# Seven products instead of eight for the columns of v, taken in turns with the plain blocks of the input projection

## The chip, the cores and the metric

The kernel runs on one core of one Trainium2 chip. The metric is device time in microseconds (us); lower is better. A kernel's time is the median of its runs, and one further execution is profiled. Engines are named as in the profile: PE is TensorE's matmuls and PEld its weight loads, DVE is VectorE, ACT is ScalarE, POOL is GpSimd, and SP is the engine whose queue issues most of the transfers.

## What is computed

One decoder block on x of 256 x 2048, all in float32. Cut to what matters here:

```python
proj = x @ w_in
b_gate, c_gate, u, q, k, v, r, z_low = split(proj)   # 1024, 1024, 1024, 512, 512, 1024, 1024, 16 columns

y_conv = group_rms_norm(b_gate * causal_conv3(c_gate * u), conv_norm_g)
z      = z_low @ w_gate_up + gate_bias
log_a  = log_sigmoid(z) / 16
o      = chunked_linear_attention(q, k, v, log_a)     # 4 heads, chunks of 64
y_gla  = group_rms_norm(o, gla_norm_g) * silu(r)

x = layer_norm(alpha * x + concat(y_conv, y_gla) @ w_out)
x = layer_norm(alpha * x + square(relu(x @ w_ff_up)) @ w_ff_down)
```

## The kernel before, in words

**Products in three.** The 256 rows are two tiles (t = 0, 1) of 128. A float32 product is made of three products of the chip's float32r type: each operand is split into a rounded part and the remainder (`split`, L110: a copy on ACT, L111, and a subtraction on DVE, L112), and PE adds high x high, high x low and low x high (`products`, L154, the matmuls at L164, L165, L166). Weights come in chunks of two slices of K (of 128 rows each) by at most 512 columns. `raw_chunk` (L142) takes a slot of the pool `raw` (13 slots, `RAWS`) and loads it on SP's queue (L115); `parts_of` (L123) splits it into a slot of the pool `hl` (5 slots, `HL`). PE then does 2 x 3 matmuls with it for each of the two row tiles.

**The input projection.** `block` (L317) makes one block of columns: 8 chunks, 96 matmuls, with one accumulator bank per row tile (six banks in all, `accp`), and hands each finished bank to a function (`done`). The columns are laid out by `IN_COLS` and `IN_BLOCKS` (L57 to L59): q, k, the 16 columns for the gates and v stand first, 2064 columns in five blocks of 412 or 414 (`qkvz`, L344; blocks 0 to 4, tiles ps_p). Then come c, u and b for the first half of the convolution's channels, c, u and b for the second half, and r, each a block of 512 (L565 to L571 and L589; tiles ps_c, ps_u, ps_b, ps_r). Block 0 also loads and splits x, and there the order on PE, ACT, DVE and SP is forced by hand (`queue`, L370); for block 1 it stays forced on ACT and DVE, after which `queue` is cleared (L383).

**The order of later work.** A list, `lag0.soon`, holds pieces of work with a count. After every group of matmuls (one chunk for one row tile) the counts go down by one (`Lagged.after`, L181), and a piece whose count is used up is issued behind that group. Everything else is ordered by the compiler's scheduler.

**Gates.** `gates` (L324) runs for each row tile when block 2 ends: small copies on ACT, a transposition on PE (pz), a copy, a matmul (z), three activations on ACT (Abs, Exp, Ln) and one operation on DVE, all issued at once.

**Attention.** `gla(t)` (L431) is a generator with four pieces: running sums of the decays on PE (bc, be, bt at L440), exponentials on ACT (L445, L446, L449, L452) and products on DVE (L447 to L453); transpositions (pqk, L462) with copies on ACT; the scores (pss, pso) and the state (pst); and the outputs (po) with their norm. The pieces are put on the list behind the last block of v, with the counts of `GLA_WAIT` (L48, L511 to L514), so they run beside the first c block, c0.

**Convolution.** The c block is copied to SBUF (`done_c`, L529). When u is there, `done_u` (L533) multiplies it with c, writes the product to a pad in DRAM (L539) and reads it back twice, shifted by one and two rows (L540, L541). All three transfers are issued on ACT's queue. The product tile has one buffer for both row tiles. DVE then weighs and adds the three (L542 to L546). `done_b` (L548) multiplies with b and normalizes.

**The up and down stage.** `up` (L760) already makes 1024 columns of the up projection by a Strassen scheme (the Winograd variant): the operands are cut in halves, rows by row tile, K by 1024 and columns by 512. Seven products of half size, in four accumulator banks a, b, c and d, replace eight. Each product is 4 steps (chunks) of 6 matmuls. The left operands are x1's parts or sums of them, made beforehand; the right ones are raw chunks or sums of them, which DVE makes in place in the slots r11, r12, r21, r22 (L774, L779, L783, L791). The chunks of the down projection are taken in between, four for every seven steps.

Of the kernel before, what the change touches and what calls it, by code (L numbers as in the profile page):

```python
# [10 lines left out]
F32 = mybir.dt.float32  # L11
# [45 lines left out]
IN_COLS = [(C_Q, NB), (C_K, NB), (C_Z, RANK), (C_V, 2 * NB),  # L57
           (C_C, NB), (C_U, NB), (C_B, NB), (C_C + NB, NB), (C_U + NB, NB), (C_B + NB, NB), (C_R, 2 * NB)]
# [4 lines left out]
def hymba_block(ctx, tc, x, x_t, w_in, conv_w, conv_g, w_gate, gate_b, gla_g, w_out,  # L63
# [207 lines left out]

    mixT = {}


    with ExitStack() as p1:
# [36 lines left out]
        vs = [keep.tile([P, HEADS, HV], F32, name=f"v_{t}") for t in range(NT)]  # L312
        las = [keep.tile([P, HEADS * HK], F32, name=f"la_{t}") for t in range(NT)]
# [10 lines left out]
        def gates(t, zl_ps):  # L324
            nc.scalar.copy(zparts[:, 0, :RANK], zl_ps)
            nc.scalar.copy(zparts[:, 1, :RANK], zl_ps)
            nc.vector.tensor_sub(zparts[:, 2, :RANK], zl_ps, zparts[:, 0, :RANK].bitcast(F32))
            pz = misc_tile(f"pz_{t}")
            nc.tensor.transpose(pz[:3 * ZP, :P], flat(zparts.bitcast(F32)), ident)
            nc.scalar.copy(zlT, pz[:3 * ZP, :P])  # L330
            z = misc_tile(f"z_{t}")
            nc.tensor.matmul(z, zlT, wgu, start=True, stop=True)
            e = las[t]
            nc.scalar.activation(e, z, AF.Abs)
            nc.scalar.activation(e, e, AF.Exp, scale=-1.0)
            nc.scalar.activation(e, e, AF.Ln, bias=one_b)
            nc.vector.scalar_tensor_tensor(las[t], z, 0.0, e, op0=ALU.min, op1=ALU.subtract)
# [6 lines left out]
        def qkvz(i):  # L344
# [8 lines left out]
            def done(t, ps):  # L353
                def go():
                    for what, d0, p0, n in pieces:
                        src = ps[:, p0:p0 + n]
                        if what == 2:
                            gates(t, src)
                        else:
                            dst = flat(vs[t]) if what == 3 else qk[t][:, what, :]  # L360
                            queued("act", lambda: nc.scalar.copy(dst[:, d0:d0 + n], src))
# [9 lines left out]
        at, ncol, done, name = qkvz(0)  # L371
# [3 lines left out]
        del queue["pe"], queue["sync"]  # L375
# [4 lines left out]


        block(*qkvz(1))
        queue.clear()  # L383


        once = tp8.tile([P, D], F32, tag="t8", name="once")
        wraw, ones, rest = once[:, 0:HEADS * HK], once[:, D - P:], once[:, D - 2 * P:D - P]
# [33 lines left out]
        for i in range(2, len(widths)):  # L421
            block(*qkvz(i))
# [98 lines left out]
        def conv_block(j):  # L521
            c_sb, h_sb = {}, {}
# [6 lines left out]
            def done_c(t, ps):  # L529
                c_sb[t] = cv.tile([P, NB], F32, tag="c", name=f"c_{j}_{t}")  # L530
                nc.scalar.copy(c_sb[t], ps)

            def done_u(t, ps):  # L533
                y = c_sb[t]
# [13 lines left out]
            def done_b(t, ps):  # L548
                y = c_sb[t]
# [13 lines left out]
            return done_c, done_u, done_b  # L563
# [28 lines left out]
    with ExitStack() as p2:  # L592
# [132 lines left out]

        KH = KT // 2
# [23 lines left out]
        def of_sum(what):  # L757
            return lambda kt: (sums[what][:, 0, kt, :], sums[what][:, 1, kt, :])

        def up(g, hT):  # L760

            n1, n2 = g * GROUP, g * GROUP + NB
            r11, r12, r21, r22 = {}, {}, {}, {}

            def raw(at, half, j, name):
                return raw_chunk(w_up, KH * half + KC * j, at, NB, f"{name}_{g}_{j}")

            def first(j):
                r11[j] = raw(n1, 0, j, "r11")
                return r11[j]  # L770

            def first_sum(j):
                r12[j] = raw(n2, 0, j, "r12")
                nc.vector.tensor_add(r11[j], r11[j], r12[j])  # L774
                return r11[j]

            def third_sum(j):
                r22[j] = raw(n2, 1, j, "r22")
                nc.vector.tensor_add(r12[j], r12[j], r22[j])  # L779
                return r12[j]  # L780

            def second_sum(j):
                nc.vector.tensor_add(r11[j], r11[j], r22[j])  # L783
                return r11[j]

            def last(j):
                r21[j] = raw(n1, 1, j, "r21")
                return r21[j]

            def fourth_sum(j):  # L790
                nc.vector.tensor_add(r11[j], r11[j], r21[j])  # L791
                return r11[j]

            def tmp(name):
                return cp.tile([P, NB], F32, tag="c", name=f"{name}_{g}")

            banks, kept = {}, {}

            def out(x, i, t, where=None):
                hidden(x if where is None else where, x, hT, i, t, f"h{g}_{i}_{t}", WAIT_UP)  # L800

            def end_1():
                kept["p1"] = tmp("p1")
                nc.scalar.copy(kept["p1"], banks["a"])

            def end_2():
                out(banks["a"], 0, 0, ht.tile([P, NB], F32, tag="relu", name=f"relu_{g}"))

            def end_6():
                kept["u"], kept["v"] = tmp("u"), tmp("v")  # L810
                nc.vector.tensor_sub(kept["u"], banks["b"], kept["p1"])
                nc.vector.tensor_sub(kept["v"], banks["c"], kept["u"])
                nc.vector.tensor_sub(kept["v"], kept["v"], banks["d"])
                out(kept["v"], 1, 1)

            def end_3():
                x = tmp("x12")
                nc.vector.tensor_sub(x, kept["u"], banks["c"])
                out(x, 1, 0)

            def end_4():
                nc.vector.tensor_add(kept["u"], banks["d"], kept["u"])
                out(kept["u"], 0, 1)

            plan = [(first, of_x1(0, 0), "a", end_1),
                    (first_sum, of_sum("s1"), "c", None),
                    (third_sum, of_sum("s3"), "d", None),
                    (second_sum, of_sum("q"), "b", end_6),
                    (lambda j: r22[j], of_sum("s4"), "c", end_3),
                    (last, of_x1(1, 0), "a", end_2),  # L830
                    (fourth_sum, of_x1(1, 1), "d", end_4)]
            n = KH // KC
            steps = [(p, j) for p in range(len(plan)) for j in range(n)]
            ready = {}

            def prepare(s):
                if s < len(steps):
                    p, j = steps[s]
# [158 lines left out]
```

## Time and profile before

| | |
|---|---|
| median of 3 runs | 1074.92 us (1074.33 to 1074.92) |
| the profiled execution, its own time | 1074.74 us |
| its span, first to last instruction | 1073.0 us |
| granted TensorE clock, mean | 0.997 |
| blocks 0 to 4 (q, k, gates, v) | 5.0 to 98.3 us |
| c0 with the attention beside it | 98.3 to 138.1 us |
| the other blocks up to the first of r | 138.1 to 247.8 us |

How to read the profile: "busy" is the time in which an engine works on an instruction; matmuls are pipelined, so that a matmul's own duration is longer than the time from one to the next. A group line names line, engine, operation, out<-in by the program's names, shapes and count, then busy time and the mean ns of one, then the idle time of the engine ahead of them and what ended it. A row of the windows gives a stretch in us from the span's start, its length, the busy time of each engine with the number of instructions, the granted clock, the share of the transfer engines and GB/s. A line of the timeline gives start, duration, engine and operation, and in brackets the idle time before it. A q behind an engine's name is its queue of issued transfers. Releasers are inferred from semaphores; a wait for several is put down to the one that came last.

### The profile page before, as it was taken

The numbers are of one execution on the slowest core, as the hardware profiler recorded it, in microseconds if no ns is written. First come the engines' busy times: TensorE is split into PE (matmuls) and PEld (weight loads), VectorE is DVE, ScalarE is ACT, GpSimd is POOL, SyncE is SP. The second block draws the span as 40 slices with busy tenths as digits, with TensorE's granted clock in tenths as the row PEclk, the third lists the DMA queues.
The fourth block names the chain that finished last, engine by engine and source line by source line (L and its number), as shares of the span: only waits on it lengthen the run. The fifth ranks groups of instructions, "written<-read, shape, count | busy, mean of one in ns | idle before, by whom it ended". The sixth has DMA issues, their size and how long they took to land.

```text
span 1073.0 us, 13204 instructions
## 1 busy us (share of the span) xinstructions
PE 1057.5 (99%) x4876; PEld 888.0 (83%) x4876; DVE 886.4 (83%) x1017; ACT 590.7 (55%) x685; POOL 1.4 (0%) x9
## 2 busy tenths in 40 slices
PE   9999999999999999999999999999999999999995
PEld 8999888888888878888888888888888888888885
DVE  6555557668565599999999999999999999999857
ACT  6575554434653356766556556556556656656620
POOL 0000000000000000000000000000000000000000
PEclk9999999999999999999999999999999999999998
DMA  9976358677686346366576566567567468367802
GB/s 334 317 241 215 117 160 277 202 222 229 191 335 192 118 149 243 99 230 221 176 230 213 185 208 223 175 201 234 168 196 259 137 198 274 120 201 256 299 27 78
DMA packets 69430, 218.69 MB, mean 204 GB/s; under 512 B 7219, under 2 KB 18243, under 8 KB 69110
## 3 DMA queue, kind: packets, MB, share of 16 engines
q1 hardware_dynamic: 64656, 206.87, 58.6%
q10 hardware_dynamic: 4710, 10.99, 2.9%
q8 instruction: 38, 0.62, 0.2%
q14 instruction: 26, 0.21, 0.1%
HBM read 214.67 MB, written 3.15 MB: 203 GB/s over the span
## 4 chain that ended last, share of the span: by engine, by line
PE 93%; DVE 4%; ACT 1%; issue 1%; DMA 1%; DVEq 0%; ACTq 0%
PE ps_dn L166 11%; PE ps_dn L165 10%; PE ps_dn L164 10%; PE ps_p L166 3%; PE ps_p L164 3%; PE ps_p L165 3%; PE ps_o L165 2%; PE ps_o L166 2%; PE ps_o L164 2%; PE ps_upa L164 2%; PE ps_upc L164 2%; PE ps_upa L166 2%; PE ps_upa L165 2%; PE ps_upc L166 2%; PE ps_upc L165 2%; PE ps_upd L164 2%
## 5 line engine op out<-in xcount | busy, mean ns | idle before, releaser
L111 ACT CAST hl_up<-raw_r 128x1024 fp32r<-128x1024 f32 x196 | 206.4, 1055 | 130.1 <-PE ps_dn L166 65.7
L112 DVE TENSOR_TENSOR hl_up<-raw_r,hl_up 128x1024 fp32r<-128x1024 f32 x196 | 237.0, 1219 | 9.8 <-ACT hl_up L111 9.3
L111 ACT CAST hl_dn<-raw_dn 128x1024 fp32r<-128x1024 f32 x128 | 134.5, 1054 | 117.5 <-PE ps_dn L166 96.9
L164 PE MATMUL ps_dn<-hl_dn,hT_hi 128*128 128x512 f32 x496 | 193.5, 391 | 0.0
L166 PE MATMUL ps_dn<-hl_dn,hT_lo 128*128 128x512 f32 x496 | 193.1, 389 | 0.0
L165 PE MATMUL ps_dn<-hl_dn,hT_hi 128*128 128x512 f32 x496 | 193.0, 389 | 0.0
L112 DVE TENSOR_TENSOR hl_dn<-raw_dn,hl_dn 128x1024 fp32r<-128x1024 f32 x128 | 155.8, 1220 | 16.1 <-ACT hl_dn L111 15.4
L166 PEld LDWEIGHTS ps_dn<-hl_dn,hT_lo 128*128 128x128 f32 x496 | 93.1, 188 | 19.6
L165 PEld LDWEIGHTS ps_dn<-hl_dn,hT_hi 128*128 128x128 f32 x496 | 93.1, 188 | 19.2
L164 PEld LDWEIGHTS ps_dn<-hl_dn,hT_hi 128*128 128x128 f32 x496 | 93.1, 188 | 19.1
L112 DVE TENSOR_TENSOR hl_o<-raw_o,hl_o 128x1024 fp32r<-128x1024 f32 x32 | 38.5, 1223 | 30.9 <-ACT hl_o L111 30.7
L112 DVE TENSOR_TENSOR hl_p<-raw_p,hl_p 128x824 fp32r<-128x824 f32 (+1 forms) x38 | 38.3, 1016 | 29.4 <-ACT hl_p L111 29.3
L111 ACT CAST hl_o<-raw_o 128x1024 fp32r<-128x1024 f32 x32 | 32.9, 1055 | 43.4 <-PE ps_o L166 36.7
L166 PE MATMUL ps_p<-hl_p,xT_lo 128*128 128x412 f32 (+1 forms) x152 | 53.3, 351 | 0.1
L164 PE MATMUL ps_p<-hl_p,xT_hi 128*128 128x412 f32 (+1 forms) x152 | 53.2, 350 | 0.0
L165 PE MATMUL ps_p<-hl_p,xT_hi 128*128 128x412 f32 (+1 forms) x152 | 53.0, 349 | 0.0
L111 ACT CAST hl_p<-raw_p 128x824 fp32r<-128x824 f32 (+1 forms) x38 | 33.3, 884 | 22.9 <-PE ps_p L166 21.8
L164 PE MATMUL ps_upa<-hl_up,x1T_hi 128*128 128x512 f32 x112 | 45.1, 403 | 0.0
L860 DVE SCALAR_TENSOR_TENSOR y<-y,ps_dn 128x512 f32<-128x512 f32 x62 | 41.7, 682 | 4.0 <-PE ps_dn L166 3.5
L164 PE MATMUL ps_upc<-hl_up,sum_s 128*128 128x512 f32 x112 | 44.3, 396 | 0.0
L165 PE MATMUL ps_upa<-hl_up,x1T_hi 128*128 128x512 f32 x112 | 43.7, 390 | 0.0
L166 PE MATMUL ps_upa<-hl_up,x1T_lo 128*128 128x512 f32 x112 | 43.7, 390 | 0.0
(279 smaller groups left out, 2143.3 us busy)
## 6 DMA issues: line engine op xcount, KB each, us to landing
raw_dn<-in_w_ff_down_dram SPq DMA_DIRECT2D x128, 512.0 KB, 4.2
raw_r<-in_w_ff_up_dram SPq DMA_DIRECT2D x112, 512.0 KB, 4.2
raw_o<-in_w_out_dram SPq DMA_DIRECT2D x32, 512.0 KB, 3.8
raw_p<-in_w_in_dram SPq DMA_DIRECT2D x22, 412.0 KB, 6.4
raw_c<-in_w_in_dram SPq DMA_DIRECT2D x16, 512.0 KB, 4.0
raw_u<-in_w_in_dram SPq DMA_DIRECT2D x16, 512.0 KB, 4.5
raw_b<-in_w_in_dram SPq DMA_DIRECT2D x16, 512.0 KB, 3.5
raw_r<-in_w_in_dram SPq DMA_DIRECT2D x16, 512.0 KB, 4.1
```

The costliest lines, as they stand in the source:

```text
L111: queued("act", lambda: nc.scalar.copy(hi, src))
L112: queued("dve", lambda: nc.vector.tensor_sub(lo, src, hi.bitcast(F32)))
L164: nc.tensor.matmul(ps[:, :ncol], ah, whi[:, j, cols], start=f, stop=False, skip_group_check=more)
L165: nc.tensor.matmul(ps[:, :ncol], ah, wlo[:, j, cols], start=False, stop=False, skip_group_check=more)
L166: nc.tensor.matmul(ps[:, :ncol], al, whi[:, j, cols], start=False, stop=e, skip_group_check=more)
L860: nc.vector.scalar_tensor_tensor(y[:, cols], y[:, cols], ALPHA if g == 0 else 1.0, ps, op0=ALU.mult, op1=ALU.add)
```

## The change

**The scheme as a function of its own.** The seven products move out of `up` into `strassen`, which takes the weight matrix, the two column offsets, the left operands, the sums of the left operands, a place for the first product (`temp`), places for three of the four results, and functions for what follows. `up` calls it with what it had before.

**v by the scheme.** v's 1024 columns are now laid out as two blocks of 512 and made by `strassen` from x (row tiles by halves of K) and w_in. The four sums of x that it needs are made on DVE from the raw x (`x_sum`), in slots of the pool `raw`, and split into slots of the pool `tp8`. The copy of the first product takes a slot of `raw` too. Results go straight to the tiles of v.

**c in v's old place.** The five narrow blocks now hold q, k, the gates' 16 columns and c (1024 columns), 412, 412, 412, 414 and 414 wide as before; c's banks are copied to tiles `cs`. The two blocks for c are gone.

**In turns.** Ahead of every chunk of the narrow blocks 1 to 4 and of block u0, `turn` is called, 40 times in all; 7 of 10 calls take one of the scheme's 28 steps. What is left after u0 is taken then. `x_sum` is called ahead of steps 0, 4, 8 and 12.

**Gates in stages.** `gates` is a generator now. Its first piece runs when the block's bank is ready, and its others after each of the next seven groups of matmuls; three of these are empty, between the activations and the last operation.

**Attention later.** `gla`'s pieces are put on the list behind u0, with the same counts, so they run beside block b0.

**Small moves.** The forced order ends for all engines behind block 0, and the constants of gates and attention are made there, in a slot of `raw` instead of `tp8`.

```diff
-IN_COLS = [(C_Q, NB), (C_K, NB), (C_Z, RANK), (C_V, 2 * NB),
-           (C_C, NB), (C_U, NB), (C_B, NB), (C_C + NB, NB), (C_U + NB, NB), (C_B + NB, NB), (C_R, 2 * NB)]
+IN_COLS = [(C_Q, NB), (C_K, NB), (C_Z, RANK), (C_C, 2 * NB), (C_V, 2 * NB),
+           (C_U, NB), (C_B, NB), (C_U + NB, NB), (C_B + NB, NB), (C_R, 2 * NB)]
...
+    def strassen(w, n1, n2, a_of, sums, temp, place, end_first, done, lagged, name):
...
+        plan = [(first, a_of(0, 0), "a", end_1),
+                (first_sum, of_sum("s1"), "c", None),
+                (third_sum, of_sum("s3"), "d", None),
+                (second_sum, of_sum("q"), "b", end_6),
+                (lambda j: r22[j], of_sum("s4"), "c", end_3),
+                (last, a_of(1, 0), "a", end_2),
+                (fourth_sum, a_of(1, 1), "d", end_4)]
+        n = KH // KC
+        steps = [(p, j) for p in range(len(plan)) for j in range(n)]
...
+        prepare(0)
+        for s, (p, j) in enumerate(steps):
+            _, lhs, bank, end = plan[p]
+            prepare(s + 1)
+            parts = parts_of(ready.pop(s), NB, f"{name}_{p}_{j}")
...
+            lagged.after(mm)
+            if j == n - 1 and end is not None:
+                end()
+            yield
...
+        cs = [keep.tile([P, 2, NB], F32, name=f"c_{t}") for t in range(NT)]
...
+                            stages = gates(t, src)
+                            next(stages)
+                            for n in range(1, 8):
+                                lag0.soon.append([n, lambda stages=stages: next(stages, None)])
...
-        once = tp8.tile([P, D], F32, tag="t8", name="once")
+        once = flat(rawp.tile([P, KC, NB], F32, tag="raw", name="once"))
...
+        def x_sum(what):
+            wide[what] = rawp.tile([P, KT // 2, P], F32, tag="raw", name=f"wide_{what}")
+            x = wide[what]
+            if what == "s1":
+                nc.vector.tensor_sub(x, A21, A22)
+            elif what == "s3":
+                nc.vector.scalar_tensor_tensor(x, A11, -1.0, A21, op0=ALU.mult, op1=ALU.subtract)
+            elif what == "q":
+                nc.vector.tensor_add(x, wide["s1"], A11)
+            else:
+                nc.vector.tensor_sub(x, wide["q"], A12)
+            sums0[what] = tp8.tile([P, 2, KT // 2, P], F32R, tag="t8", name=f"xsum_{what}")
+            split(sums0[what][:, 0], sums0[what][:, 1], x)
...
+        def small(name="p1"):
+            return flat(rawp.tile([P, KC, NB], F32, tag="raw", name=name))[:, :NB]
...
+        units = unit(rest_at, lambda i, t: flat(vs[t])[:, i * NB:(i + 1) * NB], "v")
+        sums_at = {0: "s1", 4: "s3", 8: "q", 12: "s4"}
+        taken, turns = 0, 0
+
+        def turn(i):
+
+            nonlocal taken, turns
+            turns += 7
+            if turns < 10:
+                return
+            turns -= 10
+            if taken in sums_at:
+                x_sum(sums_at[taken])
+            taken += 1
+            next(units, None)
+
+        for i in range(1, len(widths)):
+            block(*qkcz(i), before=turn)
...
-        for t in range(NT):
-            steps = gla(t)
-            for n in GLA_WAIT[t]:
-                lag0.soon.append([n, lambda steps=steps: next(steps, None)])
...
-            dc, du, db = conv_block(j)
-            block(rest_at + 3 * j * NB, NB, dc, f"c{j}")
-            block(rest_at + (3 * j + 1) * NB, NB, du, f"u{j}")
+            du, db = conv_block(j)
+            at = rest_at + (2 + 2 * j) * NB
+            block(at, NB, du, f"u{j}", before=turn if j == 0 else None)
             if j == 0:
+                for _ in units:
+                    pass
+                for t in range(NT):
+                    steps = gla(t)
+                    for n in GLA_WAIT[t]:
+                        lag0.soon.append([n, lambda steps=steps: next(steps, None)])
                 mixT["conv"] = t8_pair("mixT_conv")
-            block(rest_at + (3 * j + 2) * NB, NB, db, f"b{j}")
+            block(at + NB, NB, db, f"b{j}")
```

More of the change, by code (lines that the diff above doesn't have):

```diff
@@ L270, in part, with raw, first, first_sum @@
         return hi[:, kt % 8, t * P:(t + 1) * P], lo[:, kt % 8, t * P:(t + 1) * P]
+    KH = KT // 2
+    def strassen(w, n1, n2, a_of, sums, temp, place, end_first, done, lagged, name):
+        r11, r12, r21, r22 = {}, {}, {}, {}
+        def raw(at, half, j, what):
+            return raw_chunk(w, KH * half + KC * j, at, NB, f"{what}_{name}_{j}")
+        def first(j):
+            r11[j] = raw(n1, 0, j, "r11")
+            return r11[j]
+        def first_sum(j):
+            r12[j] = raw(n2, 0, j, "r12")
+            nc.vector.tensor_add(r11[j], r11[j], r12[j])
+            return r11[j]
+        def third_sum(j):
+            r22[j] = raw(n2, 1, j, "r22")
+            nc.vector.tensor_add(r12[j], r12[j], r22[j])
+            return r12[j]
+        def second_sum(j):
+            nc.vector.tensor_add(r11[j], r11[j], r22[j])
+            return r11[j]
+        def last(j):
+            r21[j] = raw(n1, 1, j, "r21")
+            return r21[j]
+        def fourth_sum(j):
+            nc.vector.tensor_add(r11[j], r11[j], r21[j])
+            return r11[j]
+        banks, kept = {}, {}
+        def end_1():
+            kept["p1"] = temp()
+            nc.scalar.copy(kept["p1"], banks["a"])
+        def end_6():
+            kept["u"], kept["v"] = place[0, 1](), place[1, 1]()
+            nc.vector.tensor_sub(kept["u"], banks["b"], kept["p1"])
+            nc.vector.tensor_sub(kept["v"], banks["c"], kept["u"])
+            nc.vector.tensor_sub(kept["v"], kept["v"], banks["d"])
+            done(1, 1, kept["v"])
+        def end_3():
+            x = place[1, 0]()
+            nc.vector.tensor_sub(x, kept["u"], banks["c"])
+            done(1, 0, x)
+        def end_2():
+            end_first(banks["a"])
+        def end_4():
+            nc.vector.tensor_add(kept["u"], banks["d"], kept["u"])
+            done(0, 1, kept["u"])
+        def of_sum(what):
+            return lambda kt: (sums[what][:, 0, kt, :], sums[what][:, 1, kt, :])
+        plan = [(first, a_of(0, 0), "a", end_1),
[7 more added lines that the diff above has]
+        steps = [(p, j) for p in range(len(plan)) for j in range(n)]
+        ready = {}
+        def prepare(s):
+            if s < len(steps):
+                p, j = steps[s]
+                ready[s] = plan[p][0](j)
+        prepare(0)
[3 more added lines that the diff above has]
+            parts = parts_of(ready.pop(s), NB, f"{name}_{p}_{j}")
+            if bank not in banks:
+                banks[bank] = acc_tile(f"ps_{name}{bank}")
+            begun = any(q[2] == bank for q in plan[:p])
+            mm = products(banks[bank], 0, NB, (list(range(KC * j, KC * j + KC)), *parts), lhs,
+                          j == 0 and not begun, j == n - 1, more=begun)
+            lagged.after(mm)
+            if j == n - 1 and end is not None:
+                end()
+            yield
@@ L755, in of_x1 @@
             return lambda kt: part(x1T, KH * half + kt, t)
-        def of_sum(what):
-            return lambda kt: (sums[what][:, 0, kt, :], sums[what][:, 1, kt, :])
         def up(g, hT):
[L762 to L794, printed above, removed]
-                return cp.tile([P, NB], F32, tag="c", name=f"{name}_{g}")
[L797 to L838, printed above, removed]
-                    ready[s] = plan[p][0](j)
-            prepare(0)
-            for s, (p, j) in enumerate(steps):
-                _, lhs, bank, end = plan[p]
-                prepare(s + 1)
-                name = f"up{g}_{p}_{j}"
-                parts = parts_of(ready.pop(s), NB, name)
-                if bank not in banks:
-                    banks[bank] = acc_tile(f"ps_up{bank}_{g}")
-                begun = any(q[2] == bank for q in plan[:p])
-                mm = products(banks[bank], 0, NB, (list(range(KC * j, KC * j + KC)), *parts), lhs,
-                              j == 0 and not begun, j == n - 1, more=begun)
-                lag.after(mm)
-                if j == n - 1 and end is not None:
-                    end()
-                yield
```

53 lines of the change are left out of this document (35 added, 18 removed).

## The prediction, made before the result was known

> **What bounds the kernel now.** I read the page first: busy time by engine, then the shares of the chain that ended last.
>
> ```profile
> span 1073.0 us, 13204 instructions
> PE 1057.5 (99%) x4876; PEld 888.0 (83%) x4876; DVE 886.4 (83%) x1017; ACT 590.7 (55%) x685; POOL 1.4 (0%) x9
> ...
> PE 93%; DVE 4%; ACT 1%; issue 1%; DMA 1%; DVEq 0%; ACTq 0%
> ```
>
> TensorE (PE) is busy 99% of the span and is 93% of the chain. Time falls only where PE gets fewer matmuls, and only if nothing new makes it wait. Then the stretches: blocks 1 and block u0 of the input projection, each with its own matmuls alone, and four longer ones with all engines.
>
> ```profile
> 25.50:43.42 17.92, 17.92 (x98) 17.92 (x97) 0.00 (x0) 1.07 (x3) 1.00 1.04 380
> ```
> ```profile
> 138.09:159.85 21.76, 21.76 (x96) 17.83 (x95) 0.30 (x1) 1.00 0.62 191
> ```
> ```profile
> core 0: us, PE busy (x) PEld busy (x) DVE busy (x) ACT busy (x) POOL busy (x), PEclk, DMA share, GB/s
> 60.00:80.00 20.00, 20.00 (x108) 19.31 (x107) 11.07 (x14) 16.79 (x30) 0.00 (x0) 1.00 0.75 253
> ...
> 98.34:138.09 39.75, 38.99 (x204) 31.95 (x204) 22.79 (x46) 25.26 (x48) 0.00 (x0) 1.00 0.37 116
> 159.85:181.61 21.76, 21.76 (x98) 18.02 (x97) 15.96 (x20) 8.32 (x8) 0.00 (x0) 1.00 0.86 258
> 480.00:1000.00 520.00, 520.00 (x2342) 430.10 (x2341) 502.56 (x498) 311.31 (x320) 0.00 (x0) 1.00 0.63 206
> ```
>
> A block is 96 matmuls (16 slices of K, 3 products, 2 row tiles); the counts above 96 in the first row are neighbours cut by its edges. So a 512-wide matmul takes 21.76/96 = 0.2267 us and a 412-wide one 17.92/96 = 0.1867 us. The granted clock is 1.00 throughout. The third stretch is c0 with the attention in it: 39.75 us, 18.0 more than a bare block. The last is the up and down stage, which already mixes a seven-product scheme with plain blocks: DVE busy 502.56 of 520 us, PE 520.00 of 520. Last, what PE waited for in the whole span:
>
> ```profile
> PE warm L97 <- DVE first L394: 1.2, 1, 1.2
> PE ps_p L164 <- ACT hl_begin L111: 1.1, 2, 0.7
> PE ps_up L166 <- DVE x1T_lo L112: 0.7, 1, 0.7
> PE bt L440 <- ACT ex L446: 0.7, 1, 0.7
> ```
>
> Two waits of 0.2 us follow below. There is almost no idle time to win back: 0.7 us in the attention, nothing at the gates. The gain must come from matmuls left out.
>
> **The matmuls.** The five narrow blocks keep their widths; they hold c where they held v, 480 matmuls before and after. The two c blocks go: 2 x 96 = 192 matmuls of 512 columns. The seven products for v come: 28 steps of 6 = 168 of 512 columns. That is 24 fewer: 24 x 0.2267 = **5.44 us less**. All of it lies on the path, since PE has no idle time there.
>
> **DVE, ACT and transfers in the new mix.** Forty chunks (blocks 1 to 4 and u0) take 28 steps among them, 7 for every 10. PE needs 32 x 12 x 0.1867 + 8 x 12 x 0.2267 + 168 x 0.2267 = 131.5 us.
>
> ```profile
> L112 DVE TENSOR_TENSOR hl_up<-raw_r,hl_up 128x1024 fp32r<-128x1024 f32 x196 | 237.0, 1219 | 9.8 <-ACT hl_up L111 9.3
> L111 ACT CAST hl_up<-raw_r 128x1024 fp32r<-128x1024 f32 x196 | 206.4, 1055 | 130.1 <-PE ps_dn L166 65.7
> L112 DVE TENSOR_TENSOR hl_p<-raw_p,hl_p 128x824 fp32r<-128x824 f32 (+1 forms) x38 | 38.3, 1016 | 29.4 <-ACT hl_p L111 29.3
> ...
> L111 ACT CAST hl_p<-raw_p 128x824 fp32r<-128x824 f32 (+1 forms) x38 | 33.3, 884 | 22.9 <-PE ps_p L166 21.8
> ```
> ```profile
> L783 DVE TENSOR_TENSOR raw_r<-raw_r,raw_r 128x1024 f32<-128x1024 f32 x28 | 34.1, 1219 | 0.0
> ...
> L812 DVE TENSOR_TENSOR v<-ps_upc,u 128x512 f32<-128x512 f32 x7 | 4.8, 684 | 0.0
> ```
>
> DVE: 32 narrow splits of 1.02, 36 wide ones of 1.22, 16 sums of weights of 1.22, four sums of x with their splits (8 x 1.22) and five combinations of banks of 0.68 (as L812): 109.3 us, or 83%. The up stage runs at 97% without a wait of PE, so I cost this at **0**; the cover is the ring of five split tiles. ACT: 32 x 0.88 + 40 x 1.06 = 71 us and some 9 of copies and gates (16.79 busy in the row of 60 to 80 us, less nine splits), 61%: 0. Weights moved stay the same. The first 12 steps load 12 chunks of 524 kB beside 17 of 422 kB in 17 x 2.24 + 12 x 1.36 = 54 us, 248 GB/s, where the row of 60 to 80 us shows 253 moved: 0, if there is room to put them.
>
> **Room: the raw ring.** Here I see the first real cost. The ring has 13 slots. From step 8 to step 11 the scheme holds 4 of r11, 5 of r12 and r22 together (one leaves as one comes), the copy p1 and the sum q: 11. Around step 8, with r12 whole and s1 not yet released, it holds 12. The plain chunks have two slots left, for a while one. A plain chunk holds its slot from the issue of its transfer to the end of its DVE split:
>
> ```profile
> DMA to landing us min/median/max: 4.0/6.2/8.4
> ```
> ```profile
> raw_p<-in_w_in_dram SPq DMA_DIRECT2D x16, 414.0 KB, 5.0
> ```
>
> (The first line is for all raw_p.) With a landing of L it holds the slot for L + 0.88 + 1.02. PE uses one plain chunk per 2.24 + 0.7 x 1.36 = 3.19 us. Steps 9 to 11 span some 3.7 chunks with two slots, steps 7 and 8 some 2 chunks with one. Behind falls 3.7 x ((L + 1.9)/2 - 3.19) + 2 x (L + 1.9 - 3.19). The split tiles ahead of PE (four, at a mean of 1.9 us of matmuls) cover 7.6 us. So PE waits when L is above 4.8 us, and 3.85 us for each further us of L. The rows lie on both sides: 4.0 is the shortest of raw_p, 6.2 its median. I take 5.0, the 414-wide ones, since those were loaded nearest to that time: **0.8 us more**, ends 0 and 5.4 (L = 6.2). A gain is excluded: before has no wait for weights there.
>
> The Trainium skill, "DMA: Bandwidth & Descriptors", Anatomy of one DMA, gives a fixed 2.0 us plus bytes over 436 GB/s (fitted on another issuing path): 422 kB would land in an estimated 3.0 us and the term would be 0 and the forecast 0.8 lower, 1071.5. No raw_p in this trace landed below 4.0 us, so the measured values decide.
>
> **The attention, one block later.** Its PE work is the same. In before it ran beside the c0 block, whose ends are bare copies. Now it starts right behind u0, so beside the convolution's round trips through the pad in DRAM. What these did to ACT and DVE after u0 in before (u0's matmuls end at 159.85):
>
> ```profile
> 160.27 0.35 ACTq L539 DMA_DIRECT2D pad<-h  x1
> 162.81 1.05 ACT L111 CAST hl_b<-raw_b 128x1024 fp32r<-128x1024 f32 x1 [1.71 <-PE ps_b L166]
> 165.08 0.35 ACTq L540 DMA_DIRECT2D h<-pad  x1
> 165.47 0.51 ACTq L541 DMA_DIRECT2D h<-pad  x1
> 166.07 0.39 ACTq L539 DMA_DIRECT2D pad<-h  x1
> 166.58 1.06 ACT L111 CAST hl_b<-raw_b 128x1024 fp32r<-128x1024 f32 x1 [2.72 <-DVE h L538]
> 170.89 0.33 ACTq L540 DMA_DIRECT2D h<-pad  x1
> 171.33 1.05 ACT L111 CAST hl_b<-raw_b 128x1024 fp32r<-128x1024 f32 x1 [3.69 <-PE ps_b L166]
> ```
>
> The read of the pad waits on ACT until the write has landed; ACT idles 2.72 and 3.69 us with splits queued behind (the second is put down to PE, but the read at 170.89 stands ahead of that split in ACT's order). In before this cost nothing: the b0 block ran 21.76 us, covered by the split tiles. That cover is no use to the attention, whose exponentials, products and copies run through ACT and DVE between PE's own steps. Its slack in before (c0 begins at 98.34):
>
> ```profile
> 101.80 0.59 ACT L446 ACTIVATE ex<-bc 128x512 f32<-128x512 f32 x1
> ```
> ```profile
> 102.45 0.50 PE L440 MATMUL bt<-la,rest_tile 128*128 128x512 f32 x1 [0.71 <-ACT ex L446]
> ```
> ```profile
> 103.15 0.68 DVE L450 TENSOR_TENSOR ex<-qk,ex 64x512 f32<-64x512 f32 x1
> ```
> ```profile
> 106.22 0.27 PE L462 MATMUL pqk<-ident,ex 128*128 128x128 f32 x1
> ```
>
> bt has no slack: the exponential L446 starts 3.46 us into the block, and PE waits 0.71 for it. The pad's landing comes 5.23 us after u0's end (165.08 - 159.85) and two reads are issued then (0.35 + 0.51). If they stand ahead of L446, it starts 2.6 us later and bt with it. The transposes have 2.4 us (103.83 to 106.22) and would be behind by then anyhow, so the second idle time falls into that shift in part. Ends: 0, and 2.72 + 3.69 = 6.4 with nothing hidden. I take **2.0 us more**, nearest to the one shift of 2.6 at less than certainty that the reads stand ahead. A gain is bounded by the 0.7 that bt waits now.
>
> **The rest.** The gates in stages remove no wait that PE has: 0; what hides their ACT work is the same ring. Clearing the forced order after block 0 instead of block 1; the constants, traced ahead of block 1 and held in a raw slot (their small transfers on ACT's queue and their masks on POOL already ran during block 0 in before); the convolution's rows on SP's queue, which stay as far ahead of their use; the moved function of the up stage: 0 together, since none of it is waited for by PE in the list above, and the split ring covers a short delay. Four accumulators and two plain banks fit the six banks.
>
> **Sum.** 1074.74 us is the profiled execution's own time (span 1073.0 and 1.7 around it). 1074.74 - 5.44 + 0.8 + 2.0 = 1072.1. The median of the runs, 1074.92, is 0.18 above that execution: **1072.3 us**. What a measurement of this kernel can tell from no change is about 0.2%, 2.15 us, so faster means below 1072.8.
>
> **Rivals.** *Everything hidden.* The ring holds and the scheduler sets the attention's ACT work ahead of the pad's reads: 1074.92 - 5.44 = 1069.5. For it: the up stage's faultless mix. Against it: 11 or 12 of 13 slots held.
>
> *The gain is eaten, within the bound.* ACT and DVE are emptied in the order of their lists, so both idle times fall on the attention: 1074.92 - 5.44 + 6.4 + 0.8 = 1076.7; with the first and half the second, 4.6 in place of 6.4, 1074.9. For it: the split at 166.58 that stood behind a wait it did not need. Against: the second shift is partly the first. The Trainium skill, "TensorE: Matmul & The Clock Gate", Architectural detail, says that ScalarE's and VectorE's queues are strict first in, first out; the trace agrees in that row, and the rule speaks against putting the attention there.
>
> *Slower: the raw ring runs dry* between the fourth chunk of block 2 and the second of block 3. Price as above: at L = 6.6, 3.85 x 1.8 = 6.9 us, with the attention's 2.0 it is 1078.4. It decides from L = 6.3 on, where 5.44 is used up by 2.15. For it: raw_p's median of 6.2. Against: those were landings while SP ran far ahead and DMA was full (380 GB/s in the row of block 1); with few slots free, few transfers are under way.
>
> *DVE becomes the bound:* 83% against 97% that is borne; I give it no chance of its own.
>
> **Chances.** Forecast (losses of 1 to 4 us) 0.40, everything hidden 0.18, eaten 0.25, slower 0.17. Faster by over 0.2%: 0.18 and 0.32 of the first = 0.50; within: 0.08 + 0.25 = 0.33; slower: 0.17. The range leaves out most of the last and a little at the low end: 1069.3 to 1077.7. The forecast's own: 1070.5 to 1073.5.
>
> **What would show it.** Block u1 began in before at
>
> ```profile
> 204.31 0.39 PE L164 MATMUL ps_u<-hl_u,xT_hi 128*128 128x512 f32 x1
> ```
>
> It should begin near 201.7 (5.44 earlier, 2.8 given back), with the 168 products of v at 0.227 us each. If PE waits for split weights between 60 and 85 us, the ring is the cause, and SP's queue then waits for DVE's split of the scheme's chunks. If PE waits at bt, pqk, pss or po beside ps_b, it is the pad. Both idle times at 0 would prove both terms wrong; a wait for DVE's sums in the 131 us would refute the cover I named.

## The result and the profile after

The changed kernel takes 1081.92 us (median of 6 runs, 1079.47 to 1084.56), the kernel before 1074.87 beside it (6 runs): ratio 1.0065, 95% interval 1.0055 to 1.0075. It is slower by 7.0 us, where 2.6 us less was forecast. The profiled execution took 1081.94 us, its span is 1080.2. First the page of the changed kernel, then what PE waited for in it (one wait of 0.2 us is left out):

```profile
span 1080.2 us, 13190 instructions
PE 1058.2 (98%) x4852; PEld 886.4 (82%) x4852; DVE 926.4 (86%) x1058; ACT 601.6 (56%) x697; POOL 1.4 (0%) x9
...
PE 57%; DVE 2%; issue 0%; DVEq 0%
```
```profile
PE ps_p L164 <- ACT hl_p L111: 3.7, 3, 1.8
PE pqk L626 <- DVE ex L612: 1.6, 1, 1.6
PE ps_p L165 <- DVE hl_p L112: 1.6, 3, 0.8
PE warm L97 <- DVE first L507: 1.2, 1, 1.2
PE ps_up L166 <- DVE x1T_lo L112: 0.7, 1, 0.7
PE ps_p L164 <- ACT hl_begin L111: 0.7, 1, 0.7
PE pqk L626 <- DVE ex L614: 0.5, 1, 0.5
PE ps_vd L164 <- ACT hl_v L111: 0.3, 1, 0.3
```

The 24 matmuls are gone (4852 for 4876), but PE's busy time has risen by 0.7 us in place of falling by 5.4: so busy time was added somewhere else. The chain could be followed back over only 59% of the span, so the early part has to be read from waits and windows. New are waits for the split weights of the narrow blocks (hl_p: 3.7 and 1.6) and for the attention's products (ex: 1.6 and 0.5); the wait at bt is gone.

The landmarks place the loss. Block u1 begins here, by the timeline of PE in the changed kernel:

```profile
210.20 0.39 PE L164 MATMUL ps_u<-hl_u,xT_hi 128*128 128x512 f32 x1
```

That is 5.9 us later than before (204.31) and 8.5 later than forecast (201.7). The first block of r begins 7.2 us later (255.01 for 247.83), and the span is 7.2 longer: all that was lost was lost ahead of r. Windows of the changed kernel (length, then each engine's busy time, granted clock, transfer share, GB/s): the interleaved stretch from block 1 to u0, b0 with the attention beside it, three pieces of the first, u1 with b1, and the later stage that mixes its own seven products with plain blocks.

```profile
25.90:168.42 142.52, 136.89 (x654) 122.47 (x653) 107.71 (x105) 80.57 (x103) 0.00 (x0) 0.99 0.69 227
168.42:210.20 41.78, 39.48 (x203) 31.62 (x202) 29.16 (x58) 25.27 (x46) 0.00 (x0) 1.00 0.53 167
```
```profile
66.75:75.00 8.25, 8.22 (x42) 7.40 (x41) 6.83 (x7) 2.71 (x3) 0.00 (x0) 1.00 0.58 169
75.00:78.20 3.20, 1.09 (x5) 0.40 (x3) 1.27 (x2) 1.82 (x2) 0.00 (x0) 1.00 0.30 121
78.20:83.50 5.30, 5.27 (x18) 4.66 (x19) 3.91 (x6) 1.85 (x7) 0.00 (x0) 0.68 0.53 157
...
89.50:97.00 7.50, 5.39 (x27) 4.47 (x26) 5.93 (x7) 7.25 (x9) 0.00 (x0) 1.00 0.60 171
```
```profile
210.20:255.01 44.81, 44.81 (x201) 36.84 (x200) 34.44 (x63) 19.78 (x24) 0.00 (x0) 1.00 0.66 207
```
```profile
480.00:1000.00 520.00, 520.00 (x2341) 430.20 (x2340) 504.10 (x499) 309.87 (x319) 0.00 (x0) 1.00 0.62 204
```

The first row should have been 131.5 us by the prediction's count and is 142.5: PE idles 5.6 us of it, and its busy time is too long as well. The pieces show both. From 75.00 to 78.20 PE works 1.09 of 3.20 us; right behind that the granted clock is 0.68, and 18 matmuls fill 5.30 us. From 89.50 to 97.00 PE works 5.39 of 7.50 us, at a clock of 1.00. The second row is the attention: 41.78 us where it took 39.75 beside c0. The last row is as before.

What the transfers do at that time, by the timelines of SP's queue and of ACT in the changed kernel:

```profile
69.53 0.33 SPq L115 DMA_DIRECT2D raw_r_v<-in_w_in_dram  x1
70.58 0.54 SPq L115 DMA_DIRECT2D raw_p<-in_w_in_dram  x1
71.74 0.33 SPq L115 DMA_DIRECT2D raw_r_v<-in_w_in_dram  x1
78.31 9.97 SPq L115 DMA_DIRECT2D raw_p<-in_w_in_dram  x4
```
```profile
76.36 0.88 ACT L111 CAST hl_p<-raw_p 128x824 fp32r<-128x824 f32 x1 [5.91 <-DMA raw_p<-in_w_in_dram]
77.14 1.04 ACT L111 CAST hl_v<-raw_r_v 128x1024 fp32r<-128x1024 f32 x1
```

Between 71.74 and 78.31 SP issues nothing. The narrow chunk issued at 70.58 is split by ACT at 76.36 and by DVE until 78.28, and only that frees the slot for the next narrow chunk, at 78.31: 7.7 us a chunk, where PE uses one in 3.19. An earlier stop, by the same two views:

```profile
35.71 0.37 SPq L115 DMA_DIRECT2D raw_r_v<-in_w_in_dram  x1
45.68 0.54 SPq L115 DMA_DIRECT2D raw_p<-in_w_in_dram  x1
```
```profile
42.86 0.59 ACT L322 COPY p<-ps_va 128x512 f32<-128x512 f32 x1 [6.20 <-PE ps_va L166]
43.34 1.05 ACT L111 CAST xsum_s<-wide_s 128x1024 fp32r<-128x1024 f32 x1
```

From 35.71 to 45.68 no load is issued: ACT stands 6.20 us at the copy of the first product, whose matmuls are not done, the split of the sum s3 stands behind it, and SP's next load waits for the slot of that sum (9.5 us by the waits of SP's queue).

### The profile page after: what moved, and what is told of

Same layout as the page of the kernel before. It is cut to its first block, busy times and chain, and to the rows that moved or that the text cites. A ratio compares the mean times of both kernels' runs of the same rounds, so it can differ in the third digit from the quotient of the medians.

```text
span 1080.2 us, 13190 instructions
## 1 busy us (share of the span) xinstructions
PE 1058.2 (98%) x4852; PEld 886.4 (82%) x4852; DVE 926.4 (86%) x1058; ACT 601.6 (56%) x697; POOL 1.4 (0%) x9
## 4 chain that ended last, share of the span: by engine, by line
PE 57%; DVE 2%; issue 0%; DVEq 0%
PE ps_dn L166 10%; PE ps_dn L165 10%; PE ps_dn L164 10%; PE pt_h L225 1%; DVE hl_up L112 1%; PE ps_last L166 0%; PE ps_last L165 0%; PE ps_last L164 0%; PE ps_up7a L164 0%; PE ps_up6a L164 0%; PE ps_up4a L164 0%; PE ps_up3a L164 0%; PE ps_up5c L164 0%; PE ps_up2c L164 0%; PE ps_up5a L164 0%; PE ps_up2a L164 0%
## 5 line engine op out<-in xcount | busy, mean ns | idle before, releaser
L111 ACT CAST hl_up<-raw_r_up 128x1024 fp32r<-128x1024 f32 x196 | 206.4, 1054 | 130.2 <-PE ps_dn L166 65.7
L112 DVE TENSOR_TENSOR hl_up<-raw_r_up,hl_up 128x1024 fp32r<-128x1024 f32 x196 | 236.6, 1217 | 9.8 <-ACT hl_up L111 9.4
L112 DVE TENSOR_TENSOR hl_v<-raw_r_v,hl_v 128x1024 fp32r<-128x1024 f32 x28 | 34.2, 1221 | 9.0 <-ACT hl_v L111 8.7
L111 ACT CAST hl_v<-raw_r_v 128x1024 fp32r<-128x1024 f32 x28 | 29.4, 1050 | 16.8 <-PE ps_p L166 9.0
L298 DVE TENSOR_TENSOR raw_r_up<-raw_r_up,raw_r_up 128x1024 f32<-128x1024 f32 x28 | 33.9, 1218 | 0.2
L303 DVE TENSOR_TENSOR raw_r_up<-raw_r_up,raw_r_up 128x1024 f32<-128x1024 f32 x28 | 34.1, 1217 | 0.0
```

The lines of the kernel that those rows point to most:

```text
L111: queued("act", lambda: nc.scalar.copy(hi, src))
L112: queued("dve", lambda: nc.vector.tensor_sub(lo, src, hi.bitcast(F32)))
```

## The experiments

Theory A, formed on these views: the raw ring is too short for what is lent from it, four sums of x and the copy of the first product. Rivals: B, the added vector and scalar work or its order (the copy ahead of the split of s3) makes the splits late; C, the narrow blocks' loads come late because they stand behind the scheme's in SP's queue. Beside these, the attention's term. Each run is compared with the kernel before on the same chip (medians there 1074.89 to 1075.04); ratios are to it.

**1. Nothing lent.** The copy takes a tile that the convolution uses later, the four sums are made in halves in tiles that the attention uses later.

```diff
-            wide[what] = rawp.tile([P, KT // 2, P], F32, tag="raw", name=f"wide_{what}")
+            tags = ("qT", "kT") if what in ("s1", "s4") else ("la0", "la1")
+            wide[what] = [tmp.tile([P, 4, P], F32, tag=tag, name=f"wide_{what}") for tag in tags]
...
-            return flat(rawp.tile([P, KC, NB], F32, tag="raw", name=name))[:, :NB]
+            return cv.tile([P, NB], F32, tag="h0", name=name, bufs=1)
```

> The changed kernel, with the copy of the first product and the four sums of x moved out of the ring of raw slots into other buffers (the sums in halves of 512 columns, so eight smaller operations for four). It computes the same. Theory A, the raw ring: the scheme holds up to 12 of 13 slots, weights arrive late, and PE waits between 40 and 97 us, some 8 us with the slower clock behind the waits. Then the waits go and the time falls by 7 to 9 us, to 1073 to 1075. Theory B, the load and order of DVE and ACT (the sums, and the copy that ACT holds until PE is done with the first product): the waits stay, within 2 us of 1081.9.

Measured: 1074.07 us (1072.82 to 1074.96), ratio 0.9992 (0.9983 to 1.0002), 7.85 below the changed kernel. Windows of this run, the interleaved stretch and b0 with the attention:

```profile
25.90:159.17 133.27, 133.24 (x652) 121.30 (x652) 106.12 (x108) 81.47 (x105) 0.00 (x0) 1.00 0.74 246
159.17:201.28 42.11, 39.50 (x204) 31.61 (x202) 29.16 (x58) 25.26 (x46) 0.00 (x0) 1.00 0.49 167
```

The stretch is 9.25 us shorter (0.2 of it because block 1 began at 25.74 in this execution and at 25.92 in the changed kernel), with DVE's and ACT's work all but the same (106.12 for 107.71, 81.47 for 80.57). Of the 9.25, 5.60 are idle time (5.63 less 0.03) and 3.65 are busy time (136.89 less 133.24). Of these 3.65, 1.7 are the lower clock: 5.30 us at 0.68 in the row from 78.20 to 83.50. Most of the other 1.9 lie, by an estimate, at the waits themselves: a 412-wide matmul counts as busy for 0.35 us where the next can start after 0.187, so the first 0.16 us of a wait counts as busy, and a shorter one does not show as idle at all. The ring it is; B as mere load falls.

**2, 3 and 4. Which of the lent slots.** Only the copy out of the ring; only the four sums; only s3.

> Only the copy of Strassen's first product leaves the raw ring (its tile is one that the convolution uses later); the four x sums keep their ring slots. Theory A1 (the loss comes from the number of slots lent, sums and copy alike, each for its own time): the copy's slot is held from the first to the last product, the sums' slots some 6 to 12 us each, so about a third of the 7.9 us that the kernel without any borrowed slot won: 1079 us. Theory A2 (it is the sum s3's slot behind ScalarE's copy that stops the transfers, so the copy's slot itself matters little): 1081 to 1082 us, and SP's queue still waits about 9.5 us for s3's split. Theory A3 (the copy's slot, held for 100 us, is what the ring lacks): 1075 us.

> Only the four x sums leave the raw ring (halves in tiles that attention uses later); the copy of the first product keeps its slot. A1 (every lent slot counts for its time): 1077 us. A2 (the sums' slots, above all s3's behind ScalarE's copy): 1074 to 1075 us, no wait of SP's queue for the sum's split left. A3 (the copy's slot held for 100 us): 1080 us.

> The changed kernel with the sum s3 alone out of the raw ring (two halves in tiles that attention uses later); the other three sums and the copy of the first product keep their slots. If s3's slot is what stopped the transfers, this gives most of the 7.0 us that all four sums out gave: 1075 to 1077 us. If each lent slot counts alike, one of four gives a quarter: 1079 to 1080.5 us.

Measured: the copy alone 1079.41 us (ratio 1.0043, 1.0028 to 1.0058), 2.5 below the changed kernel; the sums alone 1074.92 (1.0002, 0.9992 to 1.0011), 7.0 below; s3 alone 1080.70 (1.0058, 1.0043 to 1.0073), 1.2 below. The copy alone fits A1, the sums alone fit A2's figure and not A1's, and s3 alone lies just above the case of equal shares. No single slot is the culprit: the sums bring most, s3 less than a quarter of that (1.2 of 7.0), and the gains do not add up (2.5 and 7.0 against 7.85 together). That the copy's 2.5 fits A1 is in part luck: in the profiled execution its stretch is 5.0 us shorter (137.50 for 142.50), while b0 with the attention took 43.06 us at a granted clock of 0.96, for 41.78 at 1.00 in the changed kernel. The copy's slot is held from 42.86 to 109.45 us, 67 us and not 100. A ring of 14 slots was not run.

**5. One slot fewer.** The changed kernel with 12 slots.

```diff
-RAWS = 13
+RAWS = 12
```

> The changed kernel with 12 raw slots in place of 13. The ring theory expects a clear loss, as each slot now held for other uses comes off a shorter ring: at least 5 us more than the changed kernel, 1087 us or more, with TensorE's waits in the first 140 us grown from about 6 us to over 10. A rival that puts the loss on the vector and scalar engines' work or on the order of the blocks expects no change, 1082 us.

Measured: 1104.42 us (1.0276, 1.0260 to 1.0291), 22.5 above the changed kernel. The largest wait of PE between 20 and 156 us, and a window of it:

```profile
PE ps_p L164 <- ACT hl_p L111: 11.2, 7, 3.7
```
```profile
60.00:110.00 50.00, 35.37 (x132) 27.92 (x131) 28.91 (x30) 22.68 (x35) 0.00 (x0) 0.86 0.34 100
```

The direction was right, the size more than four times the least that was expected: in this window PE works 35.37 of 50 us, at a clock of 0.86 and with 100 GB/s moved. One slot fewer cost nearly three times what all the lent slots had cost.

**6. The order on ScalarE.** The sum s3 is made one step earlier, so that its split stands ahead of the copy; no slot is freed.

```diff
-        sums_at = {0: "s1", 4: "s3", 8: "q", 12: "s4"}
+        sums_at = {0: "s1", 3: "s3", 8: "q", 12: "s4"}
```

> The changed kernel with one number altered: the sum s3 is made one step of v earlier (with step 3, not step 4, counted from 0), so its split stands on ScalarE ahead of the copy of the first product. No slot of the ring is freed; s3's is held a little sooner. If the loss comes from the order (SP's next load waits 9.5 us for the slot of s3, whose split stands behind a copy that waits 6.2 us for TensorE), that wait falls under 4 us and the time to 1075 to 1078 us. If only the number of lent slots counts, it stays at 1081 to 1083 us.

Measured: 1081.93 us (1.0064, 1.0047 to 1.0080): no change. The wait of SP's queue for the split of a sum fell from 10.0 to 1.6 us in the stretch of 25 to 100 us, and PE's busy time between 25.9 and 60 rose from 33.17 to 34.10 us. Windows of this run, the interleaved stretch and b0 with the attention:

```profile
25.34:166.67 141.33, 136.62 (x653) 122.57 (x653) 108.17 (x105) 81.46 (x104) 0.00 (x0) 0.99 0.72 228
166.67:210.18 43.51, 40.77 (x204) 32.84 (x202) 29.27 (x58) 25.39 (x46) 0.00 (x0) 0.96 0.51 161
```

Block 1 begins at 25.34 us here and at 25.92 in the changed kernel, and b0 at 166.67 and 168.42. So the stretch takes 141.33 us for 142.50, 1.2 less, which is as much as in run 4, where s3's slot was free (141.32). The attention's block then takes 43.51 us for 41.78, at a granted clock of 0.96, and u1 begins where it did (210.18 for 210.20). So the stop at 36 to 46 us, the most striking thing in the profile, cost 1.2 of the 9.25 us (from one profiled execution of each), and in this execution the clock in a later block took more than that again. B in its second form holds for that small part. The other waits, from 73.6 us on, stayed.

**7. The order on SP's queue.** The scheme's 16 loads go on GpSimd's queue.

```diff
+            raw = rawp.tile([P, KC, NB], F32, tag="raw", name=f"raw_{what}_{name}_{j}")
+            nc.gpsimd.dma_start(raw, piece(w, kt, at, NB))
```

> The changed kernel with the 16 loads of v's chunks issued on GpSimd's queue in place of SP's; slots and counts as they are. If the plain blocks' loads come late because they stand behind the scheme's loads in SP's queue (one load that waits for its slot holds up all behind it), the loss falls: 1076 to 1079 us. If it is the number of free slots (one plain chunk after the other goes through the one slot that is left, 7.7 us from issue to issue at 70.58 and 78.31), the order of the queue changes nothing: 1080 to 1083 us.

Measured: 1088.85 us (1.0124, 1.0107 to 1.0141), 6.9 slower than the changed kernel. Neither case forecast that. Waits of the two queues in this run, GpSimd's from 10 to 140 us and SP's from 20 to 110:

```profile
POOL raw_r_v L294 <- DVE hl_p L112: 68.1, 11, 14.2
```
```profile
SPq L115 <- DVE hl_p L112: 28.9, 12, 6.3
```

The scheme's loads have a queue to themselves and wait all the same, 68.1 us, for slots that narrow chunks hold; and the narrow loads, with none of the scheme's ahead of them, wait 28.9 us on SP's queue for slots. So the order in the queue is not what makes them late. Whether a small gain of it hides behind the new loss is not shown. Of that loss 6.3 us have come about when b0 begins (174.69 us for 168.42); why two queues do worse than one was not traced.

**8 and 9. The attention beside the next block.** Attention's pieces are put on the list behind b0 in place of u0, so that they run beside u1: in the changed kernel, and in the one with nothing lent.

> The changed kernel, with the attention's pieces put behind b0 instead of u0, so beside the second u block, away from the first half's round trips through the pad. The same computation. If the round trips on ACT and DVE hold the attention's exponentials and products, the block with the attention costs about 39.8 us as in before instead of 41.8, and the time falls by about 2 us, to 1079.9. If the attention has merely become costlier beside any block of the changed order, no change: 1081.9.

> Both of the two edits above together: sums and first product out of the raw ring, attention beside the second u block. If the two losses are separate and the only ones, 1081.9 - 8 - 2 = 1072, below before by 2 to 4 us. If the ring is not the cause, 1080.

Measured: 1091.91 us (1.0155, 1.0140 to 1.0170) and 1082.78 (1.0075, 1.0060 to 1.0090): 10 and 8.7 worse, a miss. The transposes of the first convolution half now stood ahead of attention in u1, with both small PSUM banks and the last of the eight big tiles; the second row tile's attention ran only at the end of r. In the second of the two PE worked 6.26 of the 10.24 us from 308.17 to 318.41, at a granted clock of 0.50. From the waits of PE in this run:

```profile
PE ps_o L164 <- ACT hl_o L111: 4.0, 1, 4.0
PE pt_g L225 <- DVE r L747: 3.2, 3, 1.7
```

These say nothing on the pad, so the test was made again.

**10. The same, with these transposes 14 turns later, nothing lent.**

```diff
-                lag0.soon.append([1 + WAIT_C, lambda: put(y, mixT["conv"], j, t, f"c{j}{t}")])
+                lag0.soon.append([1 + WAIT_C + (14 if j == 0 else 0), lambda: put(y, mixT["conv"], j, t, f"c{j}{t}")])
```

> No borrowed ring slots, attention beside the next block (the second u block), and the transposes of the first convolution half 14 turns later, so that they stand behind attention and not ahead of it. In the run without the delay (1082.78) they held both small PSUM banks and the eighth of the shared big tiles. If that was the reason for its +8.7 us, and the pad's transfers are what attention pays beside the b block, the time is 1071.5 to 1073. If attention loses beside any block of the convolution, it is 1074 or more.

Measured: 1070.84 us (1070.57 to 1072.62), ratio 0.9966 (0.9954 to 0.9977): faster than both kernels. Windows, b0 bare and u1 with the attention:

```profile
160.21:181.97 21.76, 21.76 (x98) 18.02 (x96) 16.54 (x20) 8.24 (x8) 0.00 (x0) 1.00 0.83 266
181.97:221.94 39.97, 39.12 (x203) 31.67 (x202) 29.11 (x71) 31.67 (x54) 0.00 (x0) 1.00 0.44 144
```

The attention takes 39.97 us here, as in the kernel before (39.75), and b0 with the pad behind it is a bare block again. DVE's work in the block with the attention is the same as beside b0 with nothing lent (29.11 for 29.16 us), so the mere amount of vector work is not what made that block longer. Against the run with nothing lent the profiled executions differ by 1.4 us (1073.05 and 1071.69), the medians by 3.2.

**11. The same with the slots lent.**

> The changed kernel with its ring slots lent as they are, but attention beside the second u block and the first convolution half's transposes 14 turns later, as in the run at 1070.84. If the two losses are separate and add up, attention's 2 us come off here too and the ring's stay: 1078 to 1080 us. If moving attention back gives nothing while the ring is short, it stays at 1081 to 1083 us.

Measured: 1079.15 us (1.0040, 1.0025 to 1.0055), 2.8 below the changed kernel. The two losses are separate and add up.

**12. Before, with the attention beside b0 alone.**

> The kernel before, with one part of the change alone: the attention beside b0 instead of c0, v still by plain blocks. If the round trips through the pad hold the attention, about 2 us more than before, 1076.9, with waits of PE at the transpositions. If the cost in the changed kernel comes from something else (the scheme still running, late v), no change: 1074.9.

Measured: 1076.33 us (1.0011, 1.0002 to 1.0021); b0 with the attention took 41.06 us, 1.3 more than c0 with it. The loss is there without the scheme, at about two thirds of the size forecast, but PE waits for no transposition in this run: the longest new wait, 0.9 us, is at pst for DVE.

**13 and 14. What attention waits for beside b0.** With nothing lent, the pad's transfers go on GpSimd's queue, each row tile has a product tile of its own, and the taps are multiplied later: 5 and 6 turns, then 7 and 12.

```diff
-                nc.scalar.dma_start(h1, pad[j, 1 + t * P:1 + (t + 1) * P, :])
+                nc.gpsimd.dma_start(h1, pad[j, 1 + t * P:1 + (t + 1) * P, :])
...
+                lag0.soon.append([7 + 5 * t, taps])
```

> The kernel without borrowed ring slots (1074.07), with three edits for the convolution's way through the pad: its transfers go on GpSimd's queue, the two shifted taps are multiplied 5 and 6 turns later, and the two row tiles have a product tile each. If attention beside the convolution's second block costs 2.4 us because VectorE and ScalarE stand at the pad's transfers, those waits go: attention and that block take 39.8 us in place of 42.1, TensorE's waits for VectorE at the transposes of q and k (1.8 and 0.5 us) go, and the time is 1071.5 to 1072. If the cost comes from the mere place (more vector work in that stretch), nothing changes: 1074.

> As the run with the pad's transfers on GpSimd's queue, but the shifted taps come 7 and 12 turns later in place of 5 and 6: there VectorE stood 4.0 us at the first tap's transfer (it took until 169.69) with the split for attention's second tile behind it. If waits for the pad are what attention pays beside this block, the block takes 39.8 to 40.5 us and the time is 1071.5 to 1072.5. If it is the mere place, the block stays at 42 us and the time at 1074.

Measured: 1074.65 us (0.9998, 0.9989 to 1.0007) and 1073.37 (0.9986, 0.9976 to 0.9995). The first came out as the case of the mere place had it, but it is no proof of that: its block took 42.81 us at a granted clock of 0.96, of which some 1.7 us are the clock, and the wait that the edits were to remove was still there. The waits of DVE beside b0, in the run with nothing lent, with 5 and 6 turns, and with 7 and 12:

```profile
DVE h L699 <- DMA h<-pad: 2.7, 1, 2.7
...
DVE h L694 <- DMA pad<-h: 1.5, 1, 1.5
```
```profile
DVE h L701 <- DMA h<-pad: 4.0, 1, 4.0
```
```profile
DVE h L701 <- DMA h<-pad: 3.2, 1, 3.2
```

DVE stood at the first tap in all three, with attention's work behind it. With 7 and 12 turns, at a clock of 1.00, the block takes 40.99 us, 1.1 less than the 42.11, while a wait of 3.2 is still there, between the two cases. So about half of the attention's loss (42.11 less 39.75) went with the three edits together, and moving the attention away from the pad took nearly all of it (10). That the rest is the pad's too is likely and not shown.

## Why the prediction was wrong

**Matmuls, right.** 24 fewer, and with nothing lent the interleaved stretch is filled to 133.24 of 133.27 us.

**DVE, ACT, transfers at 0, right.** In that run PE waits for no sum of weights, with DVE busy 106 of 133 us. (With the ring short, the order on ACT did cost 1.2 us, by run 6.)

**The raw ring, wrong: the step that failed.** It was put at 0.8 us, ends 0 and 5.4; taking the lent slots out gave 7.85 by the medians and 9.25 in the stretch. The forecast let the landing decide: no wait up to 4.8 us. The landings of raw_p in the changed kernel (least, median, most):

```profile
DMA to landing us min/median/max: 3.5/4.5/7.3
```

Their median is below that limit, and PE waited. Wrong was the count of slots: "5 of r12 and r22 together" and so two left for the narrow chunks at steps 9 to 11. The scheme's loads at 69.53 and 71.74 took two of the three slots that came free then. So from 69.5 us until the split of step 10 ends at 80.55, the scheme held 12 of 13 slots and not 11: four of r11, six of r12 and r22, the copy and the sum q. The narrow chunks at 63.85, 70.58 and 78.31 follow each other at 6.7 and 7.7 us: one slot, not two. (That each of these waits comes from that count is read from the trace; that slots decide is shown by 1 to 5.) The landing had a part in it too: the chunk issued at 70.58 is taken up by ACT at 76.36, when it has landed, so some 5.8 us later and not 5.0.

The sum had a second slip. At 7 steps for every 10 chunks, three steps span 4.3 chunks and two steps 2.9; it has 3.7 and 2, without a working. With 4.3 and 2.9 the same formula gives 4.3 us at L = 5.0, in place of 0.8. A third thing was not in it at all: behind the waits the clock fell, which is 1.7 of the 9.25 us.

**The rival that came true** is the third, the ring running dry at 60 to 85 us, put at 0.17 and 1078.4: the waits are there (2.6 us of idle time from 75.1 to 85; 2.1 more come at 90 to 94 and 0.9 at 45, where it had none), with the price too low and the condition (L from 6.3) wrong. The sign named as its proof held: waits for split weights there, and SP's queue at DVE's splits, though mostly those of the narrow chunks (22.5 us from 25 to 100) and less the scheme's (4.5).

**The attention, right in size, half right in mechanism.** 2.0 us; measured 41.78 - 39.75 = 2.03, and 2.8 given back in 11. The exponential that was named (now L610) did start later, 5.14 us into the block in place of 3.46, but PE had no idle time at bt. PE waits at pqk, for products of DVE, which itself stands at the pad. By the timelines of DVE and PE in the changed kernel:

```profile
176.74 0.69 DVE L697 TENSOR_TENSOR h<-h,cw 128x512 f32<-128x512 f32 x1 [2.58 <-DMA h<-pad]
177.35 0.68 DVE L612 TENSOR_TENSOR ex<-qk,ex 128x512 f32<-128x512 f32 x1
```
```profile
178.18 0.52 PE L626 MATMUL pqk<-ident,ex 128*128 128x128 f32 x3 [1.64 <-DVE ex L612]
```

The strict order that was cited for both engines' queues agrees with these rows for DVE: the product at 177.35 comes right behind the tap that waited 2.58 us. The 2.0 came from a shift on ACT and the 2.03 from waits on DVE, so that the two figures meet is luck.

**The rest.** In the span: 7.2 = -5.44 + 9.25 + 2.03 + 1.4. Of the 1.4, 0.2 is a later first matmul (5.25 for 5.04). 0.35 lies in u1 and b1, 44.81 for 43.52: 0.94 of that difference are the transposes that stood in c1 (22.70 us against a bare 21.76). Some 0.6 are the 512-wide matmuls of v, which start every 231 to 232 ns beside narrow blocks and every 227 alone (some 20 steps of 6). What remains was not traced.

## What to carry to other kernels

Before lending slots of a load ring, count who holds each one from the issue of its load to the end of its last reader, prefetched loads included, step by step; the last free slot turns over in a full round trip (7.7 us here), and one slot fewer cost 22.5 us. Judge a striking stop by what comes due behind it, not by its length: a stop of 10 us cost 1.2 us here. Read an experiment by its stretch and its granted clock as well as by its time: in run 6 that 1.2 us could be seen only in the stretch. And when a piece is moved beside another block, count the tiles and banks that both take: the move paid only after the convolution's transposes had been put behind it.

## What the runs showed of the hardware

A wait of under 2 us can be paid twice. Behind the idle time between the matmuls at 75.10 and 77.29 us, 412-wide matmuls start every 342 to 345 ns from 79.2 to 81.6 us, in place of 187. Windows of the changed kernel, ahead of that, during it, and around a later wait of 1.70 us:

```profile
75.59:79.00 3.41, 1.41 (x6) 1.02 (x7) 1.73 (x2) 1.82 (x2) 0.00 (x0) 1.00 0.12 48
79.00:82.41 3.41, 3.41 (x11) 3.20 (x10) 2.86 (x4) 1.01 (x6) 0.00 (x0) 0.50 0.55 152
89.24:92.65 3.41, 1.71 (x9) 1.36 (x8) 1.58 (x3) 3.40 (x5) 0.00 (x0) 1.00 0.73 238
```

3.41 us at a granted clock of 0.50 cost 1.7 us, nearly as much as the idle time ahead of them (2.0). Behind the later wait the clock stays at 1.00. In run 6 it falls to 0.50 for 3.41 us behind a wait of 2.2 at pqk, with PE at work 1.81 of the 3.41 us ahead; so the busy share alone (1.41 and 1.81 with a fall, 1.71 without) does not tell which wait is paid again, and what does is not shown. The Trainium skill, "TensorE: Matmul & The Clock Gate", Part 1: The HAM clock gate, has the array at half its clock after an idle window of about 3.4 us, and at full clock after about as long a busy one. The trace agrees on the half and on the time back (3.41 us), and not on the idle window: here PE had worked 1.41 of 3.41 us, with no idle time longer than 1.84.
